# Hybrid attention step on one core: the first pair's partial results stay in SBUF, its third-sum product moves ahead, two late sums of x come from one unrounded sum, and the norms use three PSUM tiles

## The chip, the core and the metric

The kernel runs on one core of a Trainium2 chip. The metric is device time in microseconds (us). TensorE does matmuls and transposes (PE in the profile, PEld for its weight loads); VectorE (DVE), ScalarE (ACT) and GpSimd (POOL) do elementwise work. Only TensorE writes matmul results, and it writes them to PSUM; the other operands lie in SBUF. Each engine works through its own queue in order, and transfers here are issued almost all by SyncE (SP), also in order.

## The reference

One layer of a streaming encoder. 1024 prompt rows and 64 sample rows of x (width 1024) are normalised and projected by `w_in` to 6144 columns, split into q, k, v and a gate for each of two attention branches and two channel gates:

```python
h = rms_norm(x, norm_w) @ w_in
sb_q, sb_k, sb_v, sb_z, cb_q, cb_k, cb_v, cb_z, g_sb, g_cb = split(h)
cb_q = rms_norm(cb_q per head, q_norm_w);  cb_k = rms_norm(cb_k per head, k_norm_w)
o_sb = stick_breaking(sb_q, sb_k, sb_v);   o_cb = band_attention(cb_q, cb_k, cb_v, rel_bias)
b_sb = (o_sb * silu(sb_z)) @ w_proj_sb;    b_cb = (o_cb * silu(cb_z)) @ w_proj_cb
y = x + (sigmoid(g_sb) * b_sb + sigmoid(g_cb) * b_cb) @ w_out
```

The outputs are y and the new k and v rows of both branches, all in float32.

## The kernel before, in words

**Numbers in two parts.** Every float32 operand is split into a high part (ACT copies it with rounding) and a low part (DVE or POOL subtract the high part); a product takes three matmuls, high by high, low by high and high by low. The helper for a block of 1024 columns of weights is `split_quad`: ACT writes the high part, POOL the low one.

**Order.** The program sets the order itself: each engine runs its instructions as the code issues them. Nothing is planned or moved later.

**Four stages concern us; all lie in the first quarter of the run.**

Stage A. The rows of x arrive in tiles of 128 (`load_x`), are squared and summed on ACT (`prep_s`), scaled on DVE (`prep_a`) and transposed on TensorE (`prep_b`, 8 transposes, then ACT and DVE write the high and low parts). Between them run 18 groups of matmuls for the first 256 columns of both v matrices, blocks 0 and 1. A counter `at` numbers these matmuls; the list `READY` says at which of them the next tile is scaled, transposed and squared. A group covers half of the inner dimension: after the first 12 matmuls of a tile, ACT copies the half result out of PSUM (`evac_v`, L339), and the second 12 go on adding in the same bank, so that they wait for that copy. The copied halves of rows 0 to 511 are kept in `s1t`, written to DRAM (`d_s1`) and read back in stage C.

Stage B. Four blocks of 256 columns (k and q of the band branch), nine tiles each, 24 matmuls for a tile (16 for the sample tile). Each tile is normalised per head (`evac_nat`, `norm_nat`) and then transposed back in `post_nat` (2 transposes into the PSUM tile `pk`, of which there is one; ACT and DVE move it to `hl`). Between the tiles the code also runs `make_t` step by step: it makes sums of the four quarters of x, called t0 to t3, which the next stages multiply. Sum 0 takes three DVE operations of 544 columns, sum 1 takes two more, sum 3 two more on top (sent to DRAM, `d_t3`), and each finished sum is put into its two parts by `put_t` (ACT, then DVE L176).

Stage C. The other 256 columns of both v matrices, and the missing half of the first ones, for all prompt rows. It uses a scheme with seven products in place of eight for a two-by-two split of rows and columns; `ORDER` lists them as (matrix, product): product 1 uses t1, 2 uses t0, 4 uses t2, 5 uses t3, 6 uses x itself, and 0 stands for the sample rows. A product is 48 matmuls in four parts of 12, and `TJ` says at which parts `make_t` goes on. Sums of weights (`sum_w`, DVE, 1024 columns) and `split_quad` run between the parts. `evac_p` (DVE) adds a finished PSUM bank to the partial results in `u`; products 4 and 5 of a matrix add up in one bank, and product 5 may start only after the evacuation of product 4 has read it. The results go out from the tile `o`, of which there are two (`put_v`).

Stage D. Everything after: the remaining projections, the attention of both branches and the output projections.

In stage C before, the results of the first two products wait in PSUM (`held`) until the partial results `u` have come back from DRAM at the third product:

```python
if at == (2, 0):
    for e in held:
        evac_p(*e)
```

## Time and profile before

| | us |
|---|---|
| median of 3 runs (lowest, highest) | 1000.2 (999.29, 1000.63) |
| the profiled execution, its own time | 1001.18 |
| its span, first to last instruction | 999.3 |
| stage A, first product to end of its last one (10.06 to 52.51) | 42.45 |
| stage B (52.51 to 172.28) | 119.77 |
| stage C (172.28 to 261.72) | 89.44 |
| stage D (261.72 to 999.3) | 737.58 |
| PE busy over the span | 958.0 (96%) |
| DVE, ACT, POOL busy | 603.3, 498.4, 402.1 |

The stage limits are read from the instructions: a stage begins with the first matmul or transpose of its own and ends where the next one begins. Busy shares are means over stages with different limits, so that a stage has to be read by itself: which wait of TensorE ends last in it, and on which engine. A matmul counts as busy until its modelled end, so a slow matmul does not show as idle time but as fewer matmuls for the same time.

### The profile page before, as it was taken

Reading aid. Unit: us, or ns where it says so; the run is one execution under the profiler, and the core shown is the slowest. Engines: PE = TensorE matmul, PEld = TensorE weight load, DVE = VectorE, ACT = ScalarE, POOL = GpSimd, SP = SyncE. Lnnn points to the kernel's source line nnn. Section 1 sums busy time; section 2 is a strip of 40 time slices with the busy share of each in tenths; the row PEclk is TensorE's granted clock in tenths of the full one; section 3 lists DMA queues with packets and bytes.
Section 4 is the critical chain, followed back from the end, with each engine's and each line's share of the span. In section 5 each row is a group of like instructions: output and inputs, shape, how many; then the busy total and the mean of one; then the engine's idle time right before and its main releaser. Section 6 shows DMA issues by size and latency. Waiting matters only on the chain.

```text
span 999.3 us, 20474 instructions
## 1 busy us (share of the span) xinstructions
PE 958.0 (96%) x7547; PEld 910.0 (91%) x7547; DVE 603.3 (60%) x1168; ACT 498.4 (50%) x1151; POOL 402.1 (40%) x395
## 2 busy tenths in 40 slices
PE   8999989776999999999999999999999999999998
PEld 7998989676999999999999997888888888999998
DVE  6647785474545456453332257798578767389735
ACT  5656756122343434334333256677788776365320
POOL 2156555243544456665563210011141111586551
PEclk9999999978999999999999999999999999999999
DMA  8547564516464655555542598877889962673642
GB/s 285 175 142 268 188 215 169 174 64 220 154 192 138 179 184 178 172 171 171 177 151 66 159 283 216 209 197 220 235 246 264 255 160 78 207 231 101 196 133 92
DMA packets 177706, 182.73 MB, mean 183 GB/s; under 512 B 30713, under 2 KB 160125, under 8 KB 177478
## 3 DMA queue, kind: packets, MB, share of 16 engines
q1 hardware_dynamic: 166182, 166.53, 55.9%
q10 hardware_dynamic: 8608, 8.20, 2.5%
q0 software_dynamic: 2816, 6.69, 2.0%
q8 instruction: 60, 0.98, 0.4%
q14 instruction: 40, 0.33, 0.1%
HBM read 117.20 MB, written 64.16 MB: 181 GB/s over the span
## 4 chain that ended last, share of the span: by engine, by line
PE 74%; DMA 1%; ACT 1%; issue 0%; DVE 0%; SPq 0%; DVEq 0%; ACTq 0%
PE b L931 29%; PE b L1778 8%; PE o L1453 7%; PE z L1356 7%; PE pt L1409 6%; PE acc L1207 5%; PE b L1249 5%; PE acc L1100 5%; PE b L796 1%; DMA out_dram<-o 1%; PE acc L1821 1%; DMA t3l<-d_t 0%; PE acc L857 0%; ACT wT L1418 0%; DVE o L715 0%
## 5 line engine op out<-in xcount | busy, mean ns | idle before, releaser
L1409 PE MATMUL pt<-ident,be 128*128 128x128 f32 (+1 forms) x568 | 87.2, 277 | 0.9 <-ACT wT L1418 0.6
L1378 DVE TENSOR_TENSOR_SCAN be<-be,imp 128x128 f32<-128x128 f32 (+7 forms) x64 | 82.7, 1339 | 8.4 <-ACT be L1359 8.3
L1356 PE MATMUL z<-ks,sq 128*128 128x320 f32 (+5 forms) x384 | 87.7, 338 | 0.0
L1418 ACT ACTIVATE wT<-pt 128x512 f32<-128x512 f32 (+3 forms) x123 | 57.2, 498 | 43.8 <-PE pt L1409 43.7
L1409 PEld LDWEIGHTS pt<-ident,be 128*128 128x128 f32 (+1 forms) x568 | 66.2, 140 | 13.8 <-issue 5.1
L931 PE MATMUL b<-xm,wlox 128*128 128x256 f32 (+1 forms) x336 | 76.0, 286 | 0.0
L939 DVE TENSOR_TENSOR u<-b,s 128x256 f32<-128x256 f32 (+1 forms) x56 | 24.2, 439 | 73.1 <-PE b L931 66.3
L1356 PEld LDWEIGHTS z<-ks,sq 128*128 128x128 f32 x384 | 63.5, 190 | 2.2 <-ACT be L1359 0.8
L1453 PE MATMUL o<-wT,vp 128*64 128x256 f32 (+1 forms) x608 | 64.2, 356 | 0.0
L1453 PEld LDWEIGHTS o<-wT,vp 128*64 128x64 f32 x608 | 40.3, 136 | 22.3 <-issue 5.4
L931 PEld LDWEIGHTS b<-xm,wlox 128*128 128x128 f32 x336 | 56.8, 188 | 0.0
L1381 ACT ACTIVATE be<-be,sm 128x640 f32<-128x640 f32 (+5 forms) x68 | 47.2, 694 | 18.0 <-DVE sm L1380 17.9
L482 POOL TENSOR_TENSOR whix<-ws,whix 128x512 fp32r<-128x512 f32 x28 | 36.9, 1317 | 38.0 <-ACT whix L481 34.3
L1004 POOL DMA_DIRECT2D d_osb<-zt x20 | 10.8, 541 | 100.9 <-DVE zt L1467 68.4
L1359 ACT ACTIVATE be<-z 128x384 f32<-128x384 f32 (+6 forms) x104 | 48.2, 520 | 3.4 <-PE z L1356 2.9
L1369 ACT ACTIVATE be<-be,sm 128x640 f32<-128x640 f32 (+5 forms) x68 | 47.3, 695 | 3.7 <-DVE sm L1361 3.2
L1249 PE MATMUL b<-og,whi 128*128 128x384 f32 (+1 forms) x192 | 46.7, 327 | 0.0
L482 POOL TENSOR_TENSOR wlo<-ws,wlo 128x512 fp32r<-128x512 f32 x28 | 38.8, 1387 | 18.5 <-ACT wlo L481 18.3
L482 POOL TENSOR_TENSOR wlox<-wraw,wlox 128x512 fp32r<-128x512 f32 x19 | 27.8, 1464 | 42.3 <-ACT wlox L481 42.3
L833 ACT ACTIVATE hl<-u 128x256 f32<-128x256 f32 (+1 forms) x40 | 16.9, 432 | 55.5 <-issue 16.4
L931 PE MATMUL b<-t3h,whi 128*128 128x256 f32 (+1 forms) x224 | 44.6, 289 | 0.0
L931 PE MATMUL b<-t0h,whix 128*128 128x256 f32 (+1 forms) x224 | 44.6, 289 | 0.0
(405 smaller groups left out, 3356.5 us busy)
## 6 DMA issues: line engine op xcount, KB each, us to landing
wraw<-in_w_in_dram SPq DMA_DIRECT2D x31, 512.0 KB, 4.3
wrawx<-in_w_in_dram SPq DMA_DIRECT2D x17, 512.0 KB, 4.2
sq<-d_qsbT SPq DMA_DIRECT2D x32, 192.0 KB, 4.7
sq<-d_qcbT SPq DMA_DIRECT2D x32, 192.0 KB, 5.3
xt<-in_x_prompt_dram SPq DMA_DIRECT2D x8, 512.0 KB, 5.0
d_kcbT<-hl SPq DMA_DIRECT2D x8, 512.0 KB, 5.5
d_qcbT<-hl SPq DMA_DIRECT2D x8, 512.0 KB
d_ksbT<-hl SPq DMA_DIRECT2D x16, 256.0 KB, 3.3
```

Of the source, the lines that this page charges most:

```text
L482: G.tensor_tensor(out=t[:, 1], in0=src, in1=t[:, 0].bitcast(F32), op=OP.subtract)
L931: TE.matmul(ps[:, :m], w[:, hl_, k], right[s](x)[:, k, a:b], start=s < 3 and k == 0 and e == 0, stop=k == 3 and e == 2, skip_group_check=s ...
L1100: TE.matmul(ps[:, :b - a], w[:, k], xk(x, k)[:, a:b], start=k == 0 and n == 0, stop=k == KT - 1 and n == 2)
L1207: TE.matmul(ps[:, :e - a], w[:, p, cw], g[:, a:e], start=m % 12 == 0, stop=m % 12 == 11)
L1249: TE.matmul(pp[uu][:, :n], w[:, p, uu * 128:uu * 128 + 128], g[:, a:e], start=p == 0 and m == 0, stop=p == NPAIR - 1 and m == 2)
L1356: TE.matmul(z[:, :m], s[:, e, q0:q0 + 128], ks[:, h, o + x:o + y], start=(e, h) == parts[0], stop=(e, h) == parts[-1])
L1359: A.activation(be[:r, x:y], z[:r, :m], AF.Sigmoid, scale=-0.125)
L1378: V.tensor_tensor_scan(be[:r, n - 1::-1], be[:r, n - 1::-1], im[:, ::-1], 0.0, op0=OP.mult, op1=OP.max)
L1409: TE.transpose(pt[:kr, x, :r], be[:r, kb * 128:kb * 128 + kr], ident[:r, :r])
L1418: A.activation(w[:, sl:sl + m, q0:q0 + r], pt[:, :m, :r], AF.Copy)
L1453: TE.matmul(o[hd * 64:hd * 64 + 64, c0:c1], vv[:kr, kb, hd * 64:hd * 64 + 64], wT[b, p, j, hd, s // 4][:kr, s % 4, c0:c1] if j < 4 else wT ...
L1778: TE.matmul(ps[:, t], left[s](xs_, k)[:, ts_], wt_[:, k], start=s < 3 and t == k == e == 0, stop=k == 3 and e == 2, skip_group_check=s > 2 ...
```

## The change

Eight edits come together.

1. Stage A: x has three tiles in place of four, and its loads are issued in another order. Scaling a tile has a list of its own (`SCALE`), 12 to 18 matmuls ahead of its transposes; `READY` now falls mostly between two groups. Two weight splits move to a later matmul.
2. The half results of matrix 0 stay in SBUF (`u[0, "2"]` is `s1t[0]`); only those of matrix 1 go through DRAM. The first two products of stage C are therefore evacuated when they end, and `held` is gone there.
3. `make_t` makes only sums 0 and 1 in stage B, and sends the unrounded sum 1 to DRAM (`d_t1`). In stage C each of the eight late pieces (t2 and t3, four each) is made from a fetched piece of sum 1 with two DVE operations, put into two parts at once, and followed by the fetch of the piece after the next.
4. `post_nat` in stage B takes its PSUM tile in turn from `pk` and the two banks of `psQ`, which stand idle there.
5. Product (0, 4), with t2, moves from ninth to fifth place; (1, 4) and (0, 5) change places behind it, and the jobs of `make_t` in `TJ` move with them.
6. The sums and splits of weights are issued at other parts, and those of the first matrix later in stage B.
7. The table of relative biases uses one tile `rx` and the tile `hc` in turn.
8. Two jobs of `make_t` in stage B come later by one and two tiles (`jobs_at`).

```diff
--- before.py
+++ after.py
@@ -192,27 +192,38 @@
-            if n < 3:
-                held.append((n, k, d))
+            held.append((n, k, d))
             return d
...
-        for n, k in [(n, k) for k in range(4) for n in (0, 1)] + [(2, k) for k in range(4)]:
-            if n == 1:
-                r1 = total(1, k, x(0, 1, k, 1), (m, raw[k]), (p, x(1, 1, k, 1)))
-                SP.dma_start(d_t3[k], total(3, k, x(0, 1, k, 0), (m, r1), (p, x(1, 1, k, 0))))
-            else:
-                a, b = ((0, 1), (0, 0)) if n == 0 else ((1, 1), (0, 1))
-                raw[k] = total(n, k, x(0, a[0], k, a[1]), (m, x(0, b[0], k, b[1])), (p, x(1, a[0], k, a[1])),
-                               (m, x(1, b[0], k, b[1])))
-            if n == 2 and k == 3:
+        for k in range(4):
+            d = total(0, k, x(0, 0, k, 1), (m, x(0, 0, k, 0)), (p, x(1, 0, k, 1)), (m, x(1, 0, k, 0)))
+            yield
+            SP.dma_start(d_t1[k], total(1, k, x(0, 1, k, 1), (m, d), (p, x(1, 1, k, 1))))
+            if k == 3:
                 put()
             yield
-        for k in range(4):
-            SP.dma_start(t(3, 1, k).bitcast(F32), d_t3[k])
+        late = [(n, k) for n in (2, 3) for k in range(4)]
+        got = {}
+
+        def fetch(n, k):
+            got[n, k] = pool.tile([128, HF], F32, name="d")
+            SP.dma_start(got[n, k], d_t1[k])
+
+        fetch(*late[0])
+        fetch(*late[1])
         yield
-        for k in range(4):
-            put_t([t(3, s, k) for s in range(2)], t(3, 1, k).bitcast(F32))
+        for e, (n, k) in enumerate(late):
+            d = got[n, k]
+            if n == 2:
+                V.tensor_tensor(out=d, in0=d, in1=x(0, 0, k, 0), op=m)
+                V.tensor_tensor(out=d, in0=d, in1=x(1, 0, k, 0), op=m)
+            else:
+                V.tensor_tensor(out=d, in0=x(0, 1, k, 0), in1=d, op=m)
+                V.tensor_tensor(out=d, in0=d, in1=x(1, 1, k, 0), op=p)
+            put_t([t(n, s, k) for s in range(2)], d)
+            if e + 2 < 8:
+                fetch(*late[e + 2])
             yield
...
         def load_x(t):
-            xt = p0.tile([128, D], F32, name="xt", bufs=4)
+            xt = p0.tile([128, D], F32, name="xt", bufs=3)
...
                 A.activation(s1t[i][:, t], ps, AF.Copy)
-                if t == 3:
-                    SP.dma_start(d_s1[i], s1t[i][:].rearrange("p t n -> p (t n)"))
+                if t == 3 and i:
+                    SP.dma_start(d_s1, s1t[1][:].rearrange("p t n -> p (t n)"))
...
-            pt = psK.tile([128, 2, 128], F32, name="pk")
+            n = 0 if raw1[:2] == (nb - 1, 7) else t % 3
+            pt = (psQ.tile([128, 512], F32, name=f"b2{n - 1}")[:, :256].rearrange("p (j n) -> p j n", j=2) if n else
+                  psK.tile([128, 2, 128], F32, name="pk"))
...
         prep_s(0)
         prep_a(0)
+        load_x(QO[3])
         W.hi((0, 0), 2)
         prep_s(1)
         W.lo((0, 0), V)
         prep_b(0)
         beat(3)
         prep_a(1)
+        load_x(QO[4])
         W.hi((0, 1))
         prep_s(2)
         W.lo((0, 1), V)
-        load_x(8)
-        load_x(4)
...
-
-        READY = [12, 34, 58, 84, 108, 134, 160, 186]
+        SCALE = [24, 48, 72, 96, 122, 148, 174]
+        READY = [12, 36, 60, 84, 110, 136, 162, 190]
 
         def early(at):
-            if at in READY:
-                ready(READY.index(at) + 1)
-            elif at == 40:
+            if at in SCALE:
+                p = SCALE.index(at) + 2
+                prep_a(QO[p])
+                if p + 3 < 9:
+                    load_x(QO[p + 3])
+            elif at in READY:
+                p = READY.index(at) + 1
+                prep_b(QO[p])
+                if p + 2 < 9:
+                    prep_s(QO[p + 2])
+            elif at == 62:
                 W.split((1, 0), V)
-            elif at == 72:
+            elif at == 88:
                 W.split((1, 1), V)
...
+            elif at == 200:
                 W.split((2, 1), V)
...
-        s1t = [pn.tile([128, 4, 256], F32, name=f"made{j + 1}", bufs=1) for j in range(2)]
+        s1t = [pn.tile([128, 4, 256], F32, name=f"made{j}", bufs=1) for j in (3, 2)]
...
         tms = [None] * 4
-        jobs_at = [(2, 8), (3, 3), (3, 6), (3, 8), (4, 1), (4, 3), (4, 5), (4, 7)]
+        jobs_at = [(2, 8), (3, 3), (3, 6), (3, 8), (4, 1), (4, 3), (4, 6), (5, 0)]
...
-                    elif h == 0:
-                        split_quad(made[2])
-                    else:
-                        split_quad(made[1], V)
-                        load_quad(0, 1, 0, pn, "made1", 1)
...
-                if (i, ti) == (nb - 1, 0):
+                if (i, ti) == (nb - 1, 2):
                     for n in (1, 2):
                         made[n] = pn.tile([128, 4, 256], F32, name=f"made{n}", bufs=1)
                     sum_w(made[1], quad[0, 0, 1], quad[0, 1, 1], OP.add)
-                if (i, ti) == (nb - 1, 2):
+                if (i, ti) == (nb - 1, 4):
                     sum_w(made[2], made[1], quad[0, 0, 0], OP.subtract)
-                if (i, ti) == (nb - 1, 4):
-                    sum_w(quad[0, 0, 0], quad[0, 0, 0], quad[0, 0, 1], OP.subtract)
+                if (i, ti) == (nb - 1, 5):
+                    split_quad(0, made[2])
+                if (i, ti) == (nb - 1, 7):
+                    split_quad(1, made[1], V)
+                    load_quad(0, 1, 0, pn, "made1", 1)
...
-        ORDER = [(0, 1), (0, 2), (0, 6), (0, 0), (1, 1), (1, 2), (1, 6), (1, 0), (0, 4), (0, 5), (1, 4), (1, 5)]
-        TJ = [(1, 1), (2, 1), (2, 3), (4, 1), (5, 1), (5, 3), (6, 1), (6, 2), (6, 3)]
-        BANKS = {0: "2", 2: "1", 4: "3", 5: "2", 6: "1", 8: "3", 10: "2"}
-        u, bank, held = {}, {}, []
-
-        def load_s1(j, pool):
...
+        ORDER = [(0, 1), (0, 2), (0, 6), (0, 0), (0, 4), (1, 1), (1, 2), (1, 6), (1, 0), (1, 4), (0, 5), (1, 5)]
+        TJ = [(0, 2), (1, 1), (1, 3), (2, 1), (2, 3), (7, 0), (7, 2), (9, 0), (9, 2)]
+        BANKS = {0: "2", 2: "1", 4: "3", 5: "2", 6: "1", 7: "1", 9: "2"}
+        u, banks = {(0, "2"): s1t[0]}, {}
...
         def evac_p(j, s, c, ps):
+            two = lambda v: v[:, 2 * c:2 * c + 2].rearrange("p t n -> p (t n)")
             if s < 3:
-                d = u[j, "23"[s - 1]][c]
-                V.tensor_tensor(out=d, in0=ps, in1=u[j, "2"][c], op=OP.add)
+                V.tensor_tensor(out=two(u[j, "23"[s - 1]]), in0=ps, in1=two(u[j, "2"]), op=OP.add)
...
+        def part(at):
+            nonlocal psB, nu, rw, ws, raw1
+            if at[0] == 0:
...
+            if at == (0, 2):
+                split_quad(3, quad[0, 0, 1])
...
+            elif at == (0, 3):
+                sum_w(quad[0, 1, 0], quad[0, 1, 0], made[2], OP.subtract)
+                u[0, "3"] = pn.tile([128, 4, 256], F32, name="made2", bufs=1)
+            elif at == (1, 0):
+                assert not pend
+                p1x.close()
+                open_t((2,))
...
+                split_quad(2, quad[0, 1, 0])
+            elif at == (1, 1):
+                sum_w(quad[0, 0, 0], quad[0, 0, 0], quad[0, 0, 1], OP.subtract)
+                split_quad(4, quad[0, 0, 0])
+                load_quad(1, 0, 1, wpool, "wraw", 2)
+            elif at == (1, 2):
+                p1hx.close()
+                rw = rwx.enter_context(tc.tile_pool(name="rw", bufs=1, side="right"))
+                for h, w in ((1, 1), (0, 0), (1, 0)):
+                    load_quad(1, h, w, rw, f"r{h}{w}", 1)
+                nu = ph.enter_context(tc.tile_pool(name="nu", bufs=2))
+                u[1, "2"] = nu.tile([128, 4, 256], F32, name="u2", bufs=1)
+                SP.dma_start(u[1, "2"][:].rearrange("p t n -> p (t n)"), d_s1)
+                u[1, "3"] = pn.tile([128, 4, 256], F32, name="made1", bufs=1)
+            elif at == (4, 0):
+                sum_w(quad[1, 1, 1], quad[1, 0, 1], quad[1, 1, 1], OP.add)
+                made[2] = rw.tile([128, 4, 256], F32, name="r2", bufs=1)
+                sum_w(made[2], quad[1, 1, 1], quad[1, 0, 0], OP.subtract)
+                split_quad(5, made[2])
+            elif at == (4, 2):
+                split_quad(6, quad[1, 1, 1])
+                made[3] = natx.tile([128, 4, 256], F32, name="wrawx", bufs=1)
+                sum_w(made[3], quad[1, 0, 0], quad[1, 0, 1], OP.subtract)
+            elif at == (4, 3):
+                sum_w(quad[1, 1, 0], quad[1, 1, 0], made[2], OP.subtract)
+                split_quad(7, quad[1, 1, 0])
+            elif at == (6, 0):
+                split_quad(8, quad[1, 0, 1])
+                rwx.close()
+                open_t((3,))
+            elif at == (7, 0):
+                split_quad(9, made[3])
+            elif at == (7, 3):
+                split_quad(10, quad[0, 1, 1])
+                load_quad(1, 1, 1, wpool, "wraw", 2)
+                load_raw(0)
+            elif at == (9, 2):
+                split_quad(11, quad[1, 1, 1])
+                load_raw(1)
+                load_raw(2)
+            elif at == (10, 2):
+                prep(0)
+            elif at == (11, 0):
+                ws = sx.enter_context(tc.tile_pool(name="ws", bufs=3, side="right"))
+                presum(1)
+                prep(1)
+            if at in TJ:
+                next(tjobs)
+
...
+                evac_p(j, s, c, ps)
```

The instructions move as follows at the places of which the prediction speaks. First VectorE in stage B, at the job of `make_t` after the third tile of the second norm block; `pk` and `b` are PSUM tiles, `d` a sum, `t0l` and `t1l` low parts. Before:

```order
L395 TENSOR_TENSOR hl<-pk,hl 128x2x128
L361 TENSOR_TENSOR qn<-acc,wqk 128x256
L363 TENSOR_REDUCE msn<-sqn 128x4
L192 TENSOR_TENSOR d<-xm,d 128x544
L192 TENSOR_TENSOR d<-d,xb 128x544
L176 TENSOR_TENSOR t0l<-d,t0h 128x544
L192 TENSOR_TENSOR d<-xm,d 128x544
L192 TENSOR_TENSOR d<-d,xb 128x544
L176 TENSOR_TENSOR t1l<-d,t1h 128x544
L395 TENSOR_TENSOR hl<-pk,hl 128x2x64
```

and now:

```order
L411 TENSOR_TENSOR hl<-b_1374,hl 128x2x128
L375 TENSOR_TENSOR qn<-acc,wqk 128x256
L377 TENSOR_REDUCE msn<-sqn 128x4
L192 TENSOR_TENSOR d<-xm,d 128x544
L192 TENSOR_TENSOR d<-d,xb 128x544
L176 TENSOR_TENSOR t0l<-d,t0h 128x544
L411 TENSOR_TENSOR hl<-b_1432,hl 128x2x64
L375 TENSOR_TENSOR qn<-acc,wqk 128x256
```

Six operations on sums stood in a row ahead of the move out of `pk`; now there are three.

Second, VectorE at the beginning of stage C, from the second half of product (0, 1) to the second piece of t2. `made_300` is the half result that now stays in SBUF, `wrawx` and `made_2507` are weight blocks, `r`, `b` and `acc` as in the words above:

```order
L721 TENSOR_TENSOR made_300<-b_2562,made_300 128x512
L411 TENSOR_TENSOR hl<-pk,hl 128x2x128 x2
L438 TENSOR_TENSOR made_2507<-made_2507,made_2260 128x1024
L721 TENSOR_TENSOR made_300<-b_2610,made_300 128x512
L438 TENSOR_TENSOR wrawx<-wrawx,wraw 128x1024
L219 TENSOR_TENSOR d<-d,xa 128x544
L220 TENSOR_TENSOR d<-d,xm 128x544
L176 TENSOR_TENSOR t2l<-d,t2h 128x544
L721 TENSOR_TENSOR made_2631<-acc,made_300 128x512
L219 TENSOR_TENSOR d<-d,xa 128x544
L220 TENSOR_TENSOR d<-d,xm 128x544
L176 TENSOR_TENSOR t2l<-d,t2h 128x544
```

Before, the same place read

```order
L192 TENSOR_TENSOR d<-xm,xa 128x544
L192 TENSOR_TENSOR d<-d,xb 128x544
L192 TENSOR_TENSOR d<-d,xm 128x544
L712 TENSOR_TENSOR u_2716<-b_2577,u_2716 128x512
L712 TENSOR_TENSOR u_2717<-b_2616,u_2717 128x512
L712 TENSOR_TENSOR u_2718<-acc,u_2716 128x512
L712 TENSOR_TENSOR u_2719<-acc,u_2717 128x512
```

The evacuations (L712, now L721) came together, after the partial results had been read back; now each follows its own product, and the pieces of t2 stand between them.

Third, SyncE's queue from the first load of the second matrix on; `r` are its weight blocks, `d_t` the stored pieces of sum 1, `d_s_126` the half results of matrix 1:

```order
L508 DMA wraw<-in_w_in_dram 128x4x256
L211 DMA d<-d_t_129 128x544
L508 DMA r_2704<-in_w_in_dram 128x4x256
L508 DMA r_2706<-in_w_in_dram 128x4x256
L508 DMA r_2708<-in_w_in_dram 128x4x256
L757 DMA u_2713<-d_s_126 128x1024
L211 DMA d<-d_t_130 128x544
L211 DMA d<-d_t_127 128x544
L693 DMA d_sbv<-o 128x2x256
```

Here two fetches (L211) stand ahead of and behind the loads of weights and half results, where before the four blocks `r` and the two reads of `u` followed one another with no fetch between.

More of the change, by code (lines that the diff above doesn't have):

```diff
@@ L86, in hybrid_step_kernel @@
                for p in range(NPAIR)] for b in ("sb", "cb")}
-    d_s1 = [dram.tile([128, 1024], F32, name=f"d_s1{j}") for j in range(2)]
-    d_t3 = [dram.tile([128, HF], F32, name=f"d_t3{k}") for k in range(4)]
+    d_s1 = dram.tile([128, 1024], F32, name="d_s1")
+    d_t1 = [dram.tile([128, HF], F32, name=f"d_t1{k}") for k in range(4)]
     d_rb = [dram.tile([128, 768], F32, name=f"d_rb{h}") for h in range(8)]
@@ L272, in make_rb @@
             rb = rbs[0]
-            rx = p1h.tile([128, 768], F32, name="rx", bufs=2)
+            if h % 2:
+                rx = p1.tile([128, 2, 512], F32R, name="hc", bufs=1)[:].rearrange("p s n -> p (s n)")[:, 0:768].bitcast(F32)
+            else:
+                rx = p1h.tile([128, 768], F32, name="rx", bufs=1)
             V.tensor_scalar(rx[:, 0:512], rb[:, h, 256:257].to_broadcast([128, 512]), -1.0, None, op0=OP.mult)
@@ L485, in prep @@
                 load_raw(2 * i + 4)
-        quad, comb, made = {}, [], {}
+        quad, comb, made = {}, {}, {}
         def load_quad(j, h, w, pool, name, bufs):
@@ L540, in hybrid_step_kernel @@
         pend, raw1 = [], None
-        def ready(p):
-            if p + 1 < 9:
-                prep_a(QO[p + 1])
-            prep_b(QO[p])
-            if p + 2 < 9:
-                prep_s(QO[p + 2])
-            if p + 5 < 9:
-                load_x(QO[p + 5])
         def product(ps, t, ns, k, n, first, last):
@@ L718, in hybrid_step_kernel @@
+        rwx = ExitStack()
         for q, (j, s) in enumerate(ORDER):
             if s == 0:
-                sample(j, 0, comb[3 + 4 * j])
+                sample(j, 0, comb[q])
                 continue
@@ L723, in hybrid_step_kernel @@
             for c in range(2):
+                if s != 5:
+                    banks[j, c] = None
                 for tt in range(2):
[L725 to L785 removed]
@@ L786, in hybrid_step_kernel @@
-                    if at == (2, 0):
-                        for e in held:
-                            evac_p(*e)
-                    if at in TJ:
-                        next(tjobs)
+                    part((q, 2 * c + tt))
                     if tt == 0 and s != 5:
-                        bank[c] = psF.tile([128, 512], F32, name="acc") if q == 1 else bank_of(BANKS[q], c)
-                    o = bank[c][:, 256 * tt:256 * tt + 256]
+                        banks[j, c] = psF.tile([128, 512], F32, name="acc") if q == 1 else bank_of(BANKS[q], c)
@@ L794, in hybrid_step_kernel @@
+                    ps = banks[j, c]
+                    o = ps[:, 256 * tt:256 * tt + 256]
                     for k in range(4):
@@ L797, in hybrid_step_kernel @@
                                       stop=k == 3 and e == 2, skip_group_check=True)
-                if q < 2:
-                    held.append((j, s, c, bank[c]))
-                else:
-                    evac_p(j, s, c, bank[c])
+                evac_p(j, s, c, ps)
             if s == 5:
```

80 lines of the change are left out of this document (10 added, 70 removed).

## The prediction

> **What bounds the kernel now.** I read the table of stages first (columns: stretch, its length, busy time and count of each engine, granted clock, DMA share, GB/s), then who waited for whom on TensorE.
>
> ```profile
> 10.06:52.51 42.45, 37.40 (x289) 36.01 (x289) 28.30 (x41) 26.53 (x53) 6.81 (x15) 0.92 0.67 216
> 52.51:172.28 119.77, 110.91 (x931) 108.89 (x929) 82.92 (x172) 73.91 (x235) 70.43 (x85) 0.99 0.57 197
> 172.28:261.72 89.44, 67.91 (x522) 66.68 (x523) 48.09 (x54) 19.14 (x32) 29.26 (x14) 0.87 0.48 159
> 261.72:999.30 737.58, 733.05 (x5765) 690.08 (x5763) 439.85 (x896) 373.39 (x824) 293.59 (x271) 1.00 0.63 180
> ...
> PE pk L390 <- DVE hl L395: 8.9, 6, 3.1
> PE b L796 <- issue: 7.5, 1, 7.5
> PE acc L691 <- DVE u L712: 6.5, 1, 6.5
> PE b L796 <- ACT whi L499: 5.4, 1, 5.4
> PE acc L554 <- ACT made L339: 3.6, 2, 1.8
> PE b L796 <- POOL wlo L501: 1.7, 1, 1.7
> ```
>
> Stage D keeps TensorE busy and is not touched: I leave it as it is. In A, B and C TensorE is the engine that works, and it stands still for 4.9, 8.9 and 21.6 us. A stall costs more than its length, since TensorE starts again at half its clock:
>
> ```profile
> 20.46:24.35 3.89, 3.89 (x23) 3.89 (x24) 2.55 (x3) 1.29 (x2) 0.54 (x1) 0.65 0.77 288
> ...
> 206.81:212.74 5.93, 5.92 (x28) 5.93 (x28) 5.93 (x5) 0.66 (x1) 2.77 (x1) 0.50 0.18 61
> 212.88:218.53 5.65, 5.65 (x50) 5.65 (x49) 5.30 (x9) 3.31 (x4) 1.62 (x1) 1.00 0.38 117
> ```
>
> At clock 0.50, 28 matmuls took 5.93 us (0.212 each); at 1.00, 50 took 5.65 (0.113), and over stage B 931 took 110.91 (0.119, a few slow ones among them). I take 0.118 (5.66 for the 48 of a product). So C without any loss is its 522 matmuls and transposes at 0.118, 61.6 us: it loses 27.8. B loses 8.9 plus about 1.5 of slow matmuls, A about 8 (4.9 idle, 3 slow). Some 46 us are to be had.
>
> **Stage A.** Two kinds of stall go.
>
> ```profile
> 14.51 1.41 DVE L298 SCALAR_TENSOR_TENSOR xn<-xt,rs,nw 128x512 f32<-128x512 f32 x2 [0.72 <-POOL rs L280]
> ...
> 15.84 0.69 DVE L317 TENSOR_TENSOR xm<-pt,xa 128x512 fp32r<-128x512 f32 x1
> ...
> 16.58 0.74 PE L554 MATMUL acc<-whi,xm 128*128 128x256 f32 x4 [1.27 <-DVE xm L317]
> ...
> 19.00 1.05 ACT L289 ACTIVATE sq<-xt 64x1024 f32<-64x1024 f32 x1
> ...
> 20.05 0.36 ACT L339 ACTIVATE made<-acc 128x256 f32<-128x256 f32 x1
> ...
> 20.46 0.74 PE L554 MATMUL acc<-whix,xm 128*128 128x256 f32 x4 [1.79 <-ACT made L339]
> ```
>
> At 16.58 the low part xm stood behind the scaling of the next tile; the scaling now comes after it (1.27 gone). At 20.46, and once more 1.80 later, the copy of the half result (L339) stood behind the work of a tile that was transposed two matmuls before the group's end. With the transposes at the border the copy is issued first, and its 0.36 lies under the eight transposes (1.0). What is late next: the split of block 1 now comes at matmul 62, behind a squaring that needs the tile loaded last, and the sample tile's scaling behind it. Walking DVE and ACT with the durations above (scaling 1.41, low part 0.68, split 1.05 and 1.22), TensorE waits 2.1 us for that tile and 1.2 for the next, and A ends at 48.3, a gain of 4.2; I charge 1.0 for slow matmuls after these gaps. **Gain 3.2**, from 0 (loads late by 3 us, or slow all along) to 6.5 (no stall left).
>
> By the Trainium skill ("TensorE: Matmul & The Clock Gate", what is actually happening) the clock drops only after an idle window of about 3.4 us. By it these two gaps would cost no clock, and A would gain 4.2. The trace does not agree: 0.65 after a gap of 1.79.
>
> **Stage B.**
>
> ```profile
> 92.93 2.82 DVE L192 TENSOR_TENSOR d<-xm,d 128x544 f32<-128x544 f32 x1
> ...
> 97.06 0.28 DVE L395 TENSOR_TENSOR hl<-pk,hl 128x128 fp32r<-128x128 f32 x1
> ...
> 92.77 2.40 POOL L141 TENSOR_TENSOR wlo<-wraw,whi 128x1024 fp32r<-128x1024 f32 x1
> ...
> 97.40 0.44 PE L390 MATMUL pk<-ident,qn 128*128 128x128 f32 x2 [2.37 <-DVE hl L395]
> ```
>
> DVE did six operations on sums in a row ahead of the move to `hl` at 97.06; the fourth (92.93) was stretched to 2.82 while POOL worked, and `pk`, the only tile, could not be emptied. Now three stand in a row, and the third ends before the POOL operation begins; two of three tiles no longer wait on `pk` at all. Per tile DVE has 1.1 us of its own work and at most 2.9 of sums against 3.05 of TensorE (26 at 0.118): three tiles carry that. The 8.9 of the row "PE pk" (six stalls, the longest 3.1) go with the 1.5 of slow matmuls, but for the last, some 1 us at the border to C, where two tiles still use `pk` in a row: it stays and grows by some 0.5, since a split of 1.22 now stands before it (8.9 + 1.5 − 1.0 − 0.5 = 8.9; I take 8.8). **Gain 8.8**, from 6 to 9.9.
>
> **Stage C, first stall.** All times T are counted from 172.28.
>
> ```profile
> 183.18 2.53 SPq L492 DMA_DIRECT2D r<-in_w_in_dram  x4
> 185.74 2.19 SPq L707 DMA_DIRECT2D u<-d_s  x2
> ...
> 194.90 1.29 DVE L712 TENSOR_TENSOR u<-b,u 128x512 f32<-128x512 f32 x2 [10.95 <-DMA u<-d_s]
> ```
>
> The half results came 9.2 us after their issue, behind 2 MB of weights, and DVE stood in between (10.95); sums, splits and TensorE followed late. This wait goes: the half results of matrix 0 are in SBUF, those of matrix 1 are first needed two products later. But the same DVE queue now has to finish t2 before T 19.8, where product (0, 4) begins, and POOL stands in its way:
>
> ```profile
> 204.58 2.77 DVE L192 TENSOR_TENSOR d<-d,xm 128x544 f32<-128x544 f32 x1
> 207.27 2.90 DVE L176 TENSOR_TENSOR t2l<-d,t2h 128x544 fp32r<-128x544 f32 x1
> ...
> 216.56 1.28 DVE L712 TENSOR_TENSOR u<-b,u 128x512 f32<-128x512 f32 x2
> ...
> 204.38 2.38 POOL L501 TENSOR_TENSOR wlo<-made,whi 128x1024 fp32r<-128x1024 f32 x1 [18.17 <-ACT whi L499]
> 206.73 2.85 POOL L501 TENSOR_TENSOR wlox<-made,whix 128x1024 fp32r<-128x1024 f32 x1
> ...
> 216.91 2.41 POOL L501 TENSOR_TENSOR wlo<-r,whi 128x1024 fp32r<-128x1024 f32 x1 [7.33 <-ACT whi L499]
> ```
>
> A DVE operation with both inputs in SBUF (0.72 alone) ends only after the POOL operation that runs; between two POOL operations DVE gets one turn. With one input in PSUM (L712, 0.64 each) it isn't held.
>
> ```profile
> 178.15 0.42 DVE L395 TENSOR_TENSOR hl<-pk,hl 128x256 fp32r<-128x256 f32 x1 [1.21 <-ACT hl L394]
> ...
> 200.68 1.21 DVE L422 TENSOR_TENSOR made<-r,r 128x1024 f32<-128x1024 f32 x1
> ...
> 203.25 1.06 ACT L499 ACTIVATE whi<-made 128x1024 fp32r<-128x1024 f32 x1 [18.56 <-DVE made L422]
> ...
> 207.38 0.66 ACT L175 ACTIVATE t2h<-d 128x544 fp32r<-128x544 f32 x1 [1.58 <-DVE d L192]
> ```
>
> The walk: DVE leaves the last norm tile at T 6.3 (178.57). The weight sum (1.21) waits for POOL's split 3 (5.2 to 7.6) and ends at 8.8; evacuation 9.5; second sum 10.6. POOL's splits 2 and 4 (2.40 each) alternate with the first two late operations: first piece of t2 done at 18.2. Evacuation and second piece (0.72 + 0.72 + ACT 0.66 with hand-over + 0.72): 22.3. The third fetch could be issued only at 18.3, when the first piece freed its tile; a fetched piece took
>
> ```profile
> r<-in_w_in_dram SPq DMA_DIRECT2D x4, 512.0 KB, 6.6
> ...
> t3l<-d_t SPq DMA_DIRECT2D x4, 272.0 KB, 5.2
> ```
>
> 5.2 to land: third piece from 23.5 to 26.4. The fourth fetch follows at 21.8, behind the `r` blocks and half results (2 MB, issued from 18.7). It lands between T 27.0 (5.2, as `t3l`) and 33.5 (as `u` behind `r`: 11.7 us from the first issue, 183.18, to use, 194.90): I take 29.5, nearer the short end, as the `r` blocks are issued 3 us before it. The piece is done at 32.4. Product (0, 4) needs the fourth piece after nine matmuls, at 20.9, so TensorE loses 11.5, and 2.3 more in slow matmuls; (0, 4) ends at 39.3 instead of 24.8 with what small waits before it cost (0.7). The next product's weights, sums (2.4), ACT (1.06) and POOL (2.40) after the evacuation, are ready at 39.0: nothing more is lost there. **Cost 14.5.**
>
> **Stage C, second stall.** Before, product (0, 5) stood 7.47 us (the row with "issue") because the evacuation of (0, 4), which shares its bank, was late on DVE. Five products lie between them now. What is late instead is the last piece of t3: its ACT half stands behind the split of the block that is loaded last, issued when POOL has finished split 10 (T 59.8), landing at 64.3 (4.3 to 5.0 for such a block by the `wraw` and `xt` rows below), split to 65.4; then POOL holds DVE until 67.7.
>
> ```profile
> wraw<-in_w_in_dram SPq DMA_DIRECT2D x31, 512.0 KB, 4.3
> ...
> xt<-in_x_prompt_dram SPq DMA_DIRECT2D x8, 512.0 KB, 5.0
> ```
>
> The piece is done at 68.4, needed at 64.0: 4.4 and 1.5 of slow matmuls, **cost 5.9**, from 0 (ACT gets to the piece first) to 8.
>
> Sum of C: 61.6 + 14.5 + 5.9 = 82.0 against 89.4, **gain 7.4**; by the ends of the bounds from −3 to 20. Removed DVE operations (four of 0.72 in all) and 0.5 MB less through DRAM lie in these walks.
>
> **The sum.** 3.2 + 8.8 + 7.4 = 19.4. The profiled execution took 1001.18 (span 999.3), which would become 981.8; the median of the runs shown lies 1.0 lower, so I predict **981 us**.
>
> **The rivals.**
> *C comes out clean.* If the fetches land in 3 us and ACT reaches the last piece of t3 before the split, the fourth piece of t2 is done near T 26 and C takes about 70: 969. For it: DMA moved only 159 GB/s in C, there is room. Against it: the POOL rows. 0.22.
> *C gains nothing.* The t2 pieces wait on fetches that land as late as `u` did (9.2 each): the third at 27.5, the fourth near 37, product (0, 4) ends at 44, and C takes 88: 988. 0.16.
> *Three tiles in PSUM don't do what they are for.* The norm stall is DVE's lag itself, so TensorE waits for `acc` banks in place of `pk`, and B stays at 119: 990. For it: DVE is busy 82.9 of 119.8. Against it: the stalls stand only at the six-fold blocks. 0.08.
> *Slower.* x with three tiles: a load can be issued only when the tile three before is scaled, and stands in SP's queue behind stores that wait for ACT. If load (5.0), squaring, rsqrt and scaling (3.5) run one after the other, a tile costs 8.5 where TensorE needs 3.6 a tile; six tiles cost 29, and the run takes 1010. It turns slower than before from 6.8 us a tile on. Against it: with three in flight the same loop is 2.8 a tile. 0.04.
>
> **How the numbers follow.** My forecast has 0.50 (975 to 986 by its own bounds). Below 967 would take all three stages near their best ends, above 992 two of the bad cases at once: range 967 to 992. A difference of 0.2% (2 us) is about what a measurement of this kernel can tell from none; faster 0.93, same 0.02, slower 0.05.
>
> **What would show it.** Right: no `pk` wait above 1.5 us in B; stage A near 45 us up to its end at 49; in C one broken-up product at t2, whose last gap ends with L176 on DVE, a wait of some 4 us at the last piece of t3, and no wait on half results from DRAM. Wrong: TensorE waiting for `acc` in B, a squaring that waits for x in A, or t2 finished before product (0, 6) ends.

## The result, and the profile after

The changed kernel takes 984.1 us (median of 4 runs, 982.1 to 986.5) against 999.9 for the kernel before on the same chip: a ratio of 0.984 (95% interval 0.982 to 0.987). The forecast was 981 (967 to 992). The profiled execution has a span of 982.0 where it had 999.3. The table of stages of the changed kernel (stretch, its length, busy time and count of each engine, clock, DMA share, GB/s):

```profile
9.49:51.01 41.52, 36.64 (x292) 35.19 (x291) 28.49 (x41) 26.78 (x53) 9.43 (x16) 0.92 0.65 210
51.01:161.22 110.21, 108.59 (x931) 107.38 (x929) 71.12 (x163) 74.17 (x237) 70.31 (x85) 1.00 0.60 209
161.22:243.97 82.75, 67.66 (x521) 65.23 (x521) 52.29 (x59) 19.46 (x30) 30.21 (x14) 0.90 0.57 186
243.97:982.00 738.03, 733.36 (x5766) 690.16 (x5764) 442.05 (x896) 373.54 (x824) 292.45 (x271) 1.00 0.63 180
```

Whom TensorE waited for in stages A, B and C (us in total, times, longest):

```profile
PE pt L322 <- DVE xn L312: 4.8, 3, 4.1
...
PE pk L406 <- DVE hl L411: 1.5, 1, 1.5
...
PE b L811 <- ACT t2h L175: 8.9, 3, 6.2
PE b L811 <- ACT t3h L175: 4.0, 1, 4.0
...
PE b L811 <- POOL wlox L517: 1.0, 1, 1.0
```

Stage by stage, forecast and measured gain: A 3.2 and 0.9; B 8.8 and 9.6; C 7.4 and 6.7; D none and −0.5; and 0.6 ahead of stage A, which is scatter (it begins at 9.5 to 10.1 in the runs below, at 10.06 before). 19.4 was forecast, 17.3 came. In stages B and C the stalls are of the kinds forecast: a single `pk` wait of 1.5 us in stage B, one product broken up at t2, one wait of 4 us at the last piece of t3, and none on half results from DRAM. In stage A two signs came out the other way. It ended at 51.0, not near 49, and a squaring waited 2.05 us for x, which the prediction had named as a sign of being wrong. One wait in stage C was not in the forecast at all, 1.0 us for GpSimd's low part of the weights of the product after (0, 4).

One execution of a kernel below, the one with t3 one job earlier, took 1884.4 us where its other three took 982.1 to 982.7; nothing kept of it says why, and its ratio leaves it out.

### The profile page after: what moved, and what is told of

The parts are those of the page before. It is cut to its first block, busy times and chain, and to the rows that moved or that the text cites. A ratio compares the mean times of both kernels' runs of the same rounds, so it can differ in the third digit from the quotient of the medians.

```text
span 982.0 us, 20507 instructions
## 1 busy us (share of the span) xinstructions
PE 954.2 (97%) x7547; PEld 905.2 (92%) x7547; DVE 598.1 (61%) x1164; ACT 499.3 (51%) x1151; POOL 404.5 (41%) x395
## 4 chain that ended last, share of the span: by engine, by line
PE 85%; DVE 5%; issue 3%; ACT 3%; DMA 1%; POOL 1%; ACTq 0%; DVEq 0%; POOLq 0%
PE b L943 30%; PE acc L560 8%; PE o L1465 7%; PE z L1368 7%; PE pt L1421 7%; PE b L1790 6%; PE acc L1219 5%; PE b L1261 5%; PE acc L1112 5%; PE b L811 3%; DMA xt<-in_x_prompt_dram 1%; PE b L560 1%; DVE d L222 1%; PE acc L1833 1%; DVE xn L312 1%
## 5 line engine op out<-in xcount | busy, mean ns | idle before, releaser
L1390 DVE TENSOR_TENSOR_SCAN be<-be,imp 128x128 f32<-128x128 f32 (+7 forms) x64 | 82.8, 1341 | 8.3 <-ACT be L1371 8.3
L1465 PEld LDWEIGHTS o<-wT,vp 128*64 128x64 f32 x608 | 40.3, 136 | 22.3 <-issue 5.4
L1393 ACT ACTIVATE be<-be,sm 128x640 f32<-128x640 f32 (+5 forms) x68 | 47.2, 694 | 17.7 <-DVE sm L1392 17.6
L498 POOL TENSOR_TENSOR whix<-ws,whix 128x512 fp32r<-128x512 f32 x28 | 36.9, 1319 | 34.6 <-ACT whix L497 29.2
L386 ACT ACTIVATE qn<-qn,rsn 128x64 f32<-128x64 f32 (+1 forms) x144 | 38.2, 339 | 11.6 <-POOL rsn L294 11.4
```

Of the source, the lines that this page charges most:

```text
L498: G.tensor_tensor(out=t[:, 1], in0=src, in1=t[:, 0].bitcast(F32), op=OP.subtract)
L1390: V.tensor_tensor_scan(be[:r, n - 1::-1], be[:r, n - 1::-1], im[:, ::-1], 0.0, op0=OP.mult, op1=OP.max)
L1465: TE.matmul(o[hd * 64:hd * 64 + 64, c0:c1], vv[:kr, kb, hd * 64:hd * 64 + 64], wT[b, p, j, hd, s // 4][:kr, s % 4, c0:c1] if j < 4 else wT ...
```

## The experiments

Each kernel is one or a few edits away from the changed kernel (one from the kernel before) and was timed in turns with the kernel before, whose median was 999.5 to 999.9 in these sets. Stages are in us, from one profiled execution each; the limits may differ by 0.2.

| kernel | A | B | C | D | median | ratio to before (95%) |
|---|---|---|---|---|---|---|
| before | 42.5 | 119.8 | 89.4 | 737.6 | 999.9 | 1 |
| changed | 41.5 | 110.2 | 82.8 | 738.0 | 984.1 | 0.984 (0.982 to 0.987) |
| one tile in the norms | 42.1 | 111.0 | 82.9 | 737.3 | 984.2 | 0.984 (0.982 to 0.986) |
| before, three tiles | 42.8 | 117.3 | 89.8 | 739.1 | 997.5 | 0.998 (0.996 to 1.000) |
| one split of A moved | 38.0 | 109.8 | 81.8 | 738.3 | 981.5 | 0.982 (0.980 to 0.984) |
| three splits of A moved | 34.1 | 109.7 | 81.2 | 737.7 | 976.0 | 0.976 (0.974 to 0.978) |
| splits 2, 4 on VectorE | 41.2 | 110.5 | 82.5 | 738.5 | 984.3 | 0.984 (0.983 to 0.986) |
| fetch ahead of `r` | 42.0 | 109.9 | 79.6 | 738.0 | 981.0 | 0.981 (0.980 to 0.982) |
| t3 one job earlier | 40.4 | 109.8 | 78.1 | 742.6 | 982.6 | 0.982 (0.981 to 0.984) |
| the same, three tiles `o` | 41.7 | 110.2 | 77.3 | 738.6 | 979.1 | 0.980 (0.978 to 0.981) |
| all together | 34.1 | 109.7 | 72.1 | 743.5 | 969.7 | 0.969 (0.967 to 0.971) |
| and three tiles `o` | 34.1 | 109.8 | 72.0 | 738.4 | 966.1 | 0.967 (0.965 to 0.968) |
| and pieces overlapped | 34.1 | 109.3 | 66.4 | 739.1 | 961.3 | 0.962 (0.961 to 0.964) |

### Stage B: the three tiles or the moved sums?

```diff
 (the changed kernel)
-            n = 0 if raw1[:2] == (nb - 1, 7) else t % 3
-            pt = (psQ.tile(... f"b2{n - 1}") ... if n else psK.tile([128, 2, 128], F32, name="pk"))
+            pt = psK.tile([128, 2, 128], F32, name="pk")
```

> The changed kernel with one edit undone: the norm transposes of stage B use the single PSUM tile pk again. Theory (both edits of stage B matter, the tiles and the shorter rows of sums): VectorE needs 1.1 us of its own and 2.2 to 4.3 of sums at the eight tiles with a job, against 3.05 of TensorE, so each job costs TensorE 0.3 to 1.5 us on pk: stage B 113 to 116 us (110.2 with three tiles), the run 987 to 990. Rival 1 (the sums moved out of stage B are the whole gain): stage B 110 to 111, the run 984 to 985. Rival 2 (the tiles are the whole gain): stage B 118 or more, the run 992 or more.

```diff
 (the kernel before)
-            pt = psK.tile([128, 2, 128], F32, name="pk")
+            n = 0 if raw1[:2] == (nb - 1, 7) else t % 3
+            pt = (psQ.tile(... f"b2{n - 1}") ... if n else psK.tile([128, 2, 128], F32, name="pk"))
```

> The kernel before with three PSUM tiles in the norms and nothing else. Theory (both matter): six sums in a row take some 7.5 us with their locks, two free tiles cover about two TensorE tiles of 3.05, so stage B is 111 to 114 us (119.8 before) and the run 992 to 995. Rival 1 (the sums are the gain): stage B 117 or more, the run 998 or more. Rival 2 (the tiles alone): stage B 110 to 111, the run 990 to 991.

In the changed kernel the first rival held. In the kernel before it held for the stage (117.3, 117 or more expected) and missed narrowly for the run (997.5, 998 or more expected). Stage B of the changed kernel with one tile:

```profile
52.09:163.04 110.95, 109.01 (x931) 107.33 (x929) 71.31 (x163) 73.86 (x236) 70.30 (x85) 1.00 0.60 208
```

and TensorE's waits in it:

```profile
PE pk L404 <- DVE hl L409: 1.9, 2, 1.2
```

Of 9.6 us the tiles bring 0.7 here: one stall of 0.75, at the only job where VectorE falls behind; the wait of 1.2 is the one at the border to stage C. The rest comes from the other edits in stage B. VectorE's 82.9 us became 71.3, the sums stand in rows of three, two jobs come later, and sums and splits of weights moved. No run takes these apart. The place of the stalls speaks for the rows: in the kernel before all five inside the stage (97.40, 113.98, 117.39, 130.40, 145.30) stand behind one of its four rows of six. The kernel before with three tiles shows what tiles alone do (TensorE's waits in stage B):

```profile
PE pk L392 <- DVE hl L397: 3.0, 1, 3.0
PE acc L556 <- DVE qn L361: 2.5, 1, 2.5
PE acc L556 <- POOL wlox L141: 0.8, 1, 0.8
```

and VectorE around the wait for `qn` there:

```profile
126.31 2.81 DVE L192 TENSOR_TENSOR d<-xm,d 128x544 f32<-128x544 f32 x1
...
130.63 0.41 DVE L361 TENSOR_TENSOR qn<-acc,wqk 128x256 f32<-128x256 f32 x1
```

With `pk` out of the way TensorE runs on until the three `acc` banks are full, and waits for the next operation in the same queue. At the third row of six the wait only changed its name, from `hl` to `qn` (3.1 us before, 2.5 now). The other rows were mostly carried: inside the stage the waits fell from about 8 to 3.3 us. But 2.1 us came back at the border to stage C, where the last two tiles still use `pk` in a row. The first line is the kernel before, the second the one with three tiles:

```profile
172.28 0.44 PE L390 MATMUL pk<-ident,qn 128*128 128x128 f32 x2 [0.93 <-DVE hl L395]
...
170.00 0.44 PE L392 MATMUL pk<-ident,qn 128*128 128x128 f32 x2 [2.96 <-DVE hl L397]
```

In all the tiles took 2.5 us off stage B there; the run is 0.2% faster (0.0 to 0.4).

### Stage A: what the sample tile waited for

```diff
-            elif at == 62:
+            elif at == 50:
                 W.split((1, 0), V)
```

> The changed kernel with the split of block 1, first half, at matmul 50 of stage A in place of 62, so that ScalarE does it ahead of the squaring that waits for a load, and VectorE's low part stands no longer between that load and the scaling of the sample tile. Theory (the 4.15 us stall in stage A is a hand-over: load, squaring, split, low part, scaling, of which the sample tile needs only the last): the stall goes, with about 2 us of slow matmuls behind it; stage A 35 to 37 us (41.5), the run 978 to 980. Rival (the loads themselves are late, three tiles are too few): the next tile stalls in its place, stage A 39 to 41.5, the run 982 to 984.

The stall of the changed kernel in VectorE's, ScalarE's and SP's rows:

```profile
25.09 1.23 DVE L141 TENSOR_TENSOR wlo<-wraw,whi 128x1024 fp32r<-128x1024 f32 x1 [3.35 <-ACT whi L134]
26.23 1.40 DVE L312 SCALAR_TENSOR_TENSOR xn<-xt,rs,nw 64x512 f32<-64x512 f32 x2
...
22.96 1.06 ACT L303 ACTIVATE sq<-xt 128x1024 f32<-128x1024 f32 x1 [2.05 <-DMA xt<-in_x_prompt_dram]
23.92 0.19 ACT L303 ACTIVATION_READ_ACCUMULATOR sq<-xt 128x1 f32 x1
24.01 1.04 ACT L134 ACTIVATE whi<-wraw 128x1024 fp32r<-128x1024 f32 x1
...
15.77 0.37 SPq L256 DMA_DIRECT2D xt<-in_x_prompt_dram  x1
```

The scaling at 26.23 needs no load and no squaring that came after 20; it stood behind a split whose high part stood behind a squaring, which waited for a load 7.2 us (15.77 to 22.96), where I had put 5.0. With the split ahead of that squaring, the load lands at the same moment (22.87 there) and the 4.15 us stall is gone. Stage A took 38.0, between theory and rival: two stalls were left, 2.0 and 1.3, each again a split standing in front of a scaling. So all three splits were moved:

```diff
-            elif at == 62:
+            elif at == 50:
                 W.split((1, 0), V)
-            elif at == 88:
+            elif at == 98:
                 W.split((1, 1), V)
...
-            elif at == 166:
+            elif at == 176:
                 W.split((2, 0), V)
```

> The changed kernel with three weight splits of stage A moved out of the way of a scaling: block 1, first half, at matmul 50 (62), block 1, second half, at 98 (88), block 2, first half, at 176 (166). Theory (what is left in stage A after the first move, 2.0 and 1.3 us, is again a split between a squaring and a scaling on ScalarE and VectorE): both stalls go with about 1 us of slow matmuls, stage A 33.7 to 35 us (38.0 with the first move alone, 41.5 without), the run 976 to 979. Rival (three tiles of x make the loads late): one of the stalls stays or moves to the next tile, stage A 36 to 38.

Stage A of this kernel:

```profile
9.47:43.61 34.14, 33.95 (x291) 33.05 (x290) 28.03 (x41) 26.44 (x53) 9.81 (x16) 1.00 0.80 255
```

TensorE is busy 33.95 of 34.14 us at full clock. One squaring still waits 1.3 us for its load (at 22.20), but TensorE does not wait for anything behind it, so three tiles of x are enough. The stage could have gained 8 us in place of 0.9.

### Stage C: lock, fetch, or VectorE's chain?

"Lock" stands for what the prediction read from its rows: a VectorE operation with both inputs in SBUF ends only after the GpSimd operation that runs beside it. VectorE, GpSimd and SP of the changed kernel at the pieces of t2:

```profile
171.64 2.93 DVE L219 TENSOR_TENSOR d<-d,xa 128x544 f32<-128x544 f32 x1
174.60 2.81 DVE L220 TENSOR_TENSOR d<-d,xm 128x544 f32<-128x544 f32 x1
178.24 0.72 DVE L176 TENSOR_TENSOR t2l<-d,t2h 128x544 fp32r<-128x544 f32 x1 [0.83 <-ACT t2h L175]
...
190.39 0.72 DVE L219 TENSOR_TENSOR d<-d,xa 128x544 f32<-128x544 f32 x1 [3.94 <-DMA d<-d_t]
...
171.15 2.83 POOL L517 TENSOR_TENSOR wlox<-made,whix 128x1024 fp32r<-128x1024 f32 x1 [2.26 <-ACT whix L515]
173.95 2.88 POOL L517 TENSOR_TENSOR wlo<-wrawx,whi 128x1024 fp32r<-128x1024 f32 x1
...
182.43 3.76 SPq L211 DMA_DIRECT2D d<-d_t  x2
```

The fourth fetch was issued at 182.43 and used at 190.39, 21.2 and 29.2 us into the stage (forecast: 21.8 and 29.5).

```diff
-                split_quad(2, quad[0, 1, 0])
+                split_quad(2, quad[0, 1, 0], V)
...
-                split_quad(4, quad[0, 0, 0])
+                split_quad(4, quad[0, 0, 0], V)
```

> The changed kernel with the low parts of splits 2 and 4 (beginning of stage C) on VectorE in place of GpSimd. Theory (a VectorE operation on two SBUF inputs waits for the GpSimd operation that runs): the two subtractions of the first late piece take 0.72 us each in place of 2.93 and 2.81. VectorE has 2.4 us more to do and waits for ScalarE's high part, so the piece ends 17 to 18 us into stage C, as now (17.7), and the time does not move: stage C 82 to 83.5 us, the run 983 to 985. Rival (the subtractions are long because loads write the memory at the same time): they keep their 2.8 us, the piece ends at 20, stage C is 84 to 86 us and the run 985 to 988.

VectorE at the first piece in this kernel:

```profile
176.05 0.72 DVE L219 TENSOR_TENSOR d<-d,xa 128x544 f32<-128x544 f32 x1
176.80 0.72 DVE L220 TENSOR_TENSOR d<-d,xm 128x544 f32<-128x544 f32 x1
178.36 0.73 DVE L176 TENSOR_TENSOR t2l<-d,t2h 128x544 fp32r<-128x544 f32 x1 [0.83 <-ACT t2h L175]
```

Without a GpSimd operation beside them the two subtractions take 0.72 each; the piece ends 17.6 us into the stage (17.7 before) and C takes 82.5. The lock is real, and taking it away there is worth nothing, since VectorE does GpSimd's work (two splits of 1.2) and waits for a high part in the time it saved.

```diff
             elif at == (1, 2):
...
-                for h, w in ((1, 1), (0, 0), (1, 0)):
-                    load_quad(1, h, w, rw, f"r{h}{w}", 1)
-                SP.dma_start(u[1, "2"] ..., d_s1)
...
+            elif at == (2, 0):
+                for h, w in ((1, 1), (0, 0), (1, 0)):
+                    load_quad(1, h, w, rw, f"r{h}{w}", 1)
+                SP.dma_start(u[1, "2"] ..., d_s1)
```

> The changed kernel with the three weight blocks r and the half results of matrix 1 issued after the fetch of the fourth piece of t2, in place of ahead of it. Theory (the largest gap of product (0, 4), 6.2 us, is the fetch behind 2 MB of loads): the fetch lands 5 us after its issue in place of 7.9, the gap is 3 to 4 us, stage C 79 to 81 us (82.75), the run 981 to 983. Rival 1 (VectorE's chain of pieces sets the end): no change, stage C 82 to 83. Rival 2 (the r blocks become late, their sums are needed by the next product): stage C 84 or more.

C took 79.6: the theory. The gap before the fourth piece fell from 6.2 to 1.9, more than expected, because the fetch now landed before VectorE was ready for it; what is left there is VectorE's chain of pieces, 3.4 us each. TensorE at the fourth piece of this kernel:

```profile
189.30 0.58 PE L812 MATMUL b<-whi,t2h 128*128 128x256 f32 x1 [1.89 <-ACT t2h L175]
```

```diff
-        TJ = [(0, 2), (1, 1), (1, 3), (2, 1), (2, 3), (7, 0), (7, 2), (9, 0), (9, 2)]
+        TJ = [(0, 2), (1, 1), (1, 3), (2, 1), (2, 3), (6, 2), (7, 0), (7, 2), (9, 0)]
```

> The changed kernel with the four pieces of t3 one job earlier each: at parts (6,2), (7,0), (7,2), (9,0). Theory (the last piece is late because VectorE's chain of pieces begins at 212.9 us, and two of them wait for GpSimd's splits 10 and 11): the last piece ends 5 us or more earlier, the gap of 4.0 us goes with 1.5 of slow matmuls; stage C 77 to 78.5 us (82.75), the run 978 to 980. Rival 1 (the prediction's: ScalarE's part of the last piece behind split 11, whose block is loaded last): the last piece stands before that split now, same gain; then ScalarE in the changed kernel's own trace must be seen busy with split 11 before that piece. Rival 2 (the fetches, or the memory of t3, which comes free only after split 8, set the pace): the gap moves to an earlier piece or stays above 2, stage C 80 to 82.5.

In stage C the gap of 4.0 became 0.9, and the stage took 78.1:

```profile
225.34 0.39 PE L811 MATMUL b<-whi,t3h 128*128 128x256 f32 x1 [0.94 <-ACT t3h L175]
```

That lies in the theory's range, with some luck: of the 4.7 us by which the stage is shorter, 3.1 are this gap, and 1.4 are two waits that the edit does not touch (the gap before the fourth piece of t2, 6.2 and now 5.8, and the wait of 1.0 for GpSimd, which did not come). The last piece in the changed kernel, whose rows decide between the theory and my forecast:

```profile
225.31 2.73 DVE L222 TENSOR_TENSOR d<-xm,d 128x544 f32<-128x544 f32 x1
...
223.94 1.05 ACT L515 ACTIVATE whix<-wraw 128x1024 fp32r<-128x1024 f32 x1
228.84 0.66 ACT L175 ACTIVATE t3h<-d 128x544 fp32r<-128x544 f32 x1 [3.85 <-DVE d L223]
```

ScalarE had finished split 11 at 225.0 and then waited 3.85 us for VectorE. The split delayed the piece by its GpSimd half, which held VectorE (2.73 for 0.72), and not by standing ahead of it on ScalarE.

But the run gained only 1.5 us (982.6, where 978 to 980 was expected), since stage D took 742.6. The rows of VectorE and SP at its border show why:

```profile
237.05 0.69 DVE L724 TENSOR_TENSOR o<-b,made 128x512 f32<-128x512 f32 x1 [5.99 <-DMA out_dram<-o]
...
239.13 0.67 DVE L463 TENSOR_TENSOR ws<-wraw 128x512 f32<-128x512 f32 x1
...
228.79 0.37 SPq L451 DMA_DIRECT2D wraw<-in_w_in_dram  x1
229.21 0.51 SPq L451 DMA_DIRECT2D wrawx<-in_w_in_dram  x1
229.76 0.51 SPq L693 DMA_DIRECT2D d_cbv<-o  x1
230.31 0.47 SPq L697 DMA_DIRECT2D out_dram<-o  x1
```

The evacuation waited for a tile `o`; there are two, and the stores that free this one had been issued behind two blocks of weights (that the blocks made them late is read from this order and not tested). Behind that evacuation stood the sums for stage D's first weights. The next run tests whether the missing tile is the cause:

```diff
 (besides the edit above, at both places)
-            v = nu.tile([128, 512], F32, name="o")
+            v = nu.tile([128, 512], F32, name="o", bufs=3)
```

> The changed kernel with the pieces of t3 one job earlier, as before, and three tiles for the results o in place of two. Theory (what the earlier pieces gained in stage C, 4.7 us, was given back at its border to stage D, 4.5 us: the evacuation of product (0, 5) waits 6 us for the store of an o tile that stands behind two loads of weights, and the sums for stage D's first weights stand behind that evacuation on VectorE): the wait goes, stage D is 738 to 739.5 us again (742.6), stage C stays at 78, the run 977 to 979 (982.6 with two tiles). Rival (the sums and splits of stage D's first weights are late by themselves, as they depend on the loads): stage D stays at 741 to 743, the run 981 to 983.

Stage D is back at 738.6, and 979.1 us came out: the theory.

### All together

The kernel of the next run has the three splits of A; split 1 one tile earlier in B; in C the sum for split 4 at part (0, 2), splits 2 and 4 on VectorE, and t3 one job earlier. The third and fourth fetch go into two tiles of their own, in a job ahead of the loads of `r`:

```diff
+                more.insert(0, dxx.enter_context(tc.tile_pool(name="dx", bufs=2)))
+                next(tjobs)
                 for h, w in ((1, 1), (0, 0), (1, 0)):
                     load_quad(1, h, w, rw, f"r{h}{w}", 1)
```

> All together: the three splits of stage A; split 1 one tile earlier at the end of stage B; in stage C the sum for split 4 two parts earlier, splits 2 and 4 on VectorE ahead of the pieces, the third and fourth fetch into two tiles of their own ahead of the weight blocks r, and the pieces of t3 one job earlier. Theory (product (0, 4) then loses only VectorE's chain of four pieces, of some 3.3 us each from 173 us on, 12 us into the stage): stage A 34 to 35, stage B 109 to 110, stage C 71 to 74 (82.75; 61.6 without any loss); 41.5 + 110.2 + 82.75 become 216 to 219, the run 966 to 969. Rival (fetches set the pace whatever the order): stage C 75 to 78, the run 970 to 973.

Stages A, B and C came out as expected (34.1, 109.7, 72.1), the run at 969.7, 0.7 us above, for the reason just shown: stage D 743.5. This run and the one with t3 alone were made together, before the third tile `o`. With it:

> All edits together, and three tiles o. Theory: stage D 738 to 739.5 us in place of 743.5, stages A to C as in the run without the third tile (34, 110, 72): the run 964 to 966. Rival: as for the other run with three tiles, 968 to 970.

966.1, at the upper end of what was expected. Product (0, 4) still lost VectorE's chain, in which each piece waits 0.7 to 0.8 us for ScalarE's high part. The last run makes the low part of a piece after the subtractions of the next:

```diff
-            put_t([t(n, s, k) for s in range(2)], d)
+            A.activation(t(n, 0, k), d, AF.Copy)
+            back.append((t(n, 1, k), d, t(n, 0, k)))
+            while len(back) > (0 if e in (3, 7) else 1):
+                lo, src, hi = back.pop(0)
+                V.tensor_tensor(out=lo, in0=src, in1=hi.bitcast(F32), op=OP.subtract)
```

> As the run with all edits and three tiles o, and besides VectorE makes the low part of a late piece only after the subtractions of the next one, so that it does not wait for ScalarE's high part (0.7 to 0.8 us a piece). Theory (product (0, 4) now loses VectorE's chain alone): four times 0.75 us less in the chain, less what it waits elsewhere, stage C 69 to 71 us (72), the run 961 to 964. Rival (the third and fourth fetch, issued 12.8 us into the stage behind a weight block, become the limit): stage C 71.5 to 72.5, no gain.

Stage C of this kernel:

```profile
153.02:219.39 66.37, 63.15 (x520) 62.30 (x521) 47.31 (x57) 19.19 (x31) 23.95 (x11) 0.97 0.66 217
```

and the largest of TensorE's waits in it:

```profile
PE b L826 <- DVE t2l L229: 2.2, 2, 2.0
```

C took 66.4, below the theory's range and 3.6 us better than its middle: the gap at the last piece of t3 (0.9) went as well, and the clock over the stage was 0.97 where it was 0.95 in both runs before. 961.3 us is 3.8% below the kernel before (interval 3.6 to 4.0) and 2.3% below the changed kernel by their medians; no run of this study was faster.

## Why the prediction was right, and where it was not

**Stage A, 3.2 forecast, 0.9 measured: a mis-sized term.** The two kinds of stall that were to go went, and the new one stood at the place and in the order of work that the prediction named (a split behind a squaring that needs the tile loaded last, the scaling behind the split). Its size was wrong: 2.1 forecast, 4.15 measured. The term that failed is the load's landing, taken as the median of its group, 5.0; this one took 7.2. Two blocks of weights had been issued ahead of it (at 13.25 and 13.68); that they made it late is likely, but no run varies it. The slow matmuls after the stall, for which 1.0 was charged, cost about 2 (26 of them took 5.2 us in place of 3.1). At the next tile, where 1.2 was forecast, TensorE did not wait; a wait of 0.5 came three tiles later (at 46.01).

**Stage B, 8.8 forecast, 9.6 measured: the right size from a half wrong reason.** The step said that two of three tiles no longer wait on `pk`, and that "three tiles carry that". One tile carries it too, but for 0.7 us. What did most of the work is the rest of the edits in that stage, most likely the first half of the same step, three operations in a row in place of six. The rival in which the tiles don't do what they are for was partly right about the tiles: in the kernel before they left 3.3 us of waits on `acc`, as it said, but they took away more than that inside the stage. Its price was wrong, since it gave the whole stall to the tiles. The remaining wait at the border to C was forecast at 1.5 and measured 1.52.

**Stage C, 7.4 forecast, 6.7 measured: the walk held.** From the start of the stage: first piece of t2 done 18.2 forecast, 17.7 measured; second 22.3 and 21.2; third 26.4 and 24.6; fourth 32.4 and 32.1; end of product (0, 4) 39.3 and 38.7. The fetch run shows that the late fetch decided the fourth piece, as the walk had it; the run with the splits on VectorE shows that the lock is what stretched the first. The third piece had its fetch ready sooner than the 5.2 taken: it was issued at 179.00 and the subtraction began at 182.93 without a wait. One term was put at nothing: after product (0, 4) "nothing more is lost", and TensorE lost 1.0 at 200.88, waiting for GpSimd's low part of the next product's weights.

**The last piece of t3: time right, cause wrong.** 4.4 and 1.5 were forecast, and 4.0 and the slow matmuls after it came. The step put it down to ScalarE's part behind split 11. ScalarE was free; VectorE's chain of four pieces, held twice by GpSimd's splits 10 and 11, was late. The forecast came close since the same walk had VectorE held until 67.7 (66.8 measured, 228.04 in the row above), and partly by luck: it counted 0.7 us from there to the end of the piece, where 2.2 passed.

**The sum.** A's gain was forecast 2.3 too high and C's 0.7, B's 0.8 too low; stage D lost 0.5, and 0.6 came ahead of stage A. That leaves 2.1 us of span, and 3 of the median, whose runs spread over 4. Errors of both signs stand in it, so the sum is better than its worst part. The slower rival (x loads one after another) had its price from a loop that never formed: with the splits moved, stage A runs with three tiles at TensorE's pace.

## What to carry to other kernels

When a buffer's wait shows on the tensor engine, ask first why the engine that empties it is late: more buffers alone brought 2.5 of 9.6 us, since part of the wait moved to the next thing in the same queue and part to the next place with a single buffer. With less work in a row on that engine the buffers hardly mattered (0.7). In a queue that runs in order, put first what already has its inputs, and judge a load by what is issued ahead of it and not by its group's median. A gain in one stage is only a gain once the next stage's first inputs are earlier too: here 4.5 us were given back until the stores had a third tile.
